# Four groups of GpSimd's element-wise work on VectorE, and an emission order that books the two engines as excluding each other

## The chip, the cores and the metric

The kernel runs on one core of one Trainium2 chip. TensorE (PE in the profile, its weight loads PEld), VectorE (DVE), ScalarE (ACT), GpSimd (POOL) and SyncE (SP) each work through a queue of their own in order, and semaphores make them wait for one another. DMA transfers are issued from the queues of SP, ACT and POOL. The metric is the device time of one execution in microseconds, as the median of several runs.

## The reference

One layer of a hybrid decoder over 1024 tokens of width 1024, all in float32, cut to what matters here:

```python
mod = silu(c) @ ada_w + ada_b
sh1, sc1, g1, sh2, sc2, g2 = split(mod, 6)
h = rms_norm(x, norm1_g) * (1 + sc1) + sh1
z = h @ w_in                                   # 1024 x 3896
y_fox = fox_mixer(z[:, :FOX_COLS])             # 8 heads of 64, attention with a forget gate
y_rwkv = rwkv7_mixer(z[:, FOX_COLS:])          # 8 heads of 64, a linear recurrence
x = x + g1 * (concat(y_fox, y_rwkv) @ w_out)
h = rms_norm(x, norm2_g) * (1 + sc2) + sh2
x = x + g2 * moe_ffn(h)                        # 64 experts of width 256, 6 per token, and a shared one
out = rms_norm(x, final_g)
# in fox_mixer, k and v are mixed with the token before:
k = a_k * shift_prev(k) + (1 - a_k) * k        # v the same with a_v; then rms_norm(k)
```

## The kernel before

Most float32 products are made as three matmuls of a high and a low part. For the weights of the input projection the function `halves` makes them: ScalarE copies the raw tile (`wraw`) into `whi` (L364), and L366 subtracts to get `wlo`, on VectorE for tile 1 and on GpSimd for the 30 others.

The projection (`proj`, L439) goes over 31 tiles of 128 columns: one of small columns, `wda`, `gd`, then r, k and v for each of four pairs of RWKV heads, four of the gate `fg`, and fk, fv and fq for each of four pairs of attention heads. Tile 0 is made at L428. Every other tile is 48 matmuls of 128x512 at L439, 1440 in all.

Around it run the other streams. For a pair of RWKV heads, in two halves each: `kappa` squares k (L630), sums the squares on TensorE (L602), takes inverse roots in a chain of tiny VectorE steps on the tile `hs` (`rstd_steps`, L152 to L164), spreads them (L610) and turns them back on TensorE (L617). `pre` makes two small products (L493). `main` scans (L671) and multiplies up to `fb` (L693), which the matmuls L698 read. `tok` transposes the results (L728). `inverse` inverts triangular blocks on VectorE (L773, L776), `merge` puts them together (L809, L820), and `chain` goes through 16 steps of the recurrence (L879 for its products, L910 to L943 for a step). For a pair of attention heads `fk` and `fv` mix with the token before (L1009 to L1013, L1037 to L1041); `fk` and `fq` normalise through the same chain (L602 to L617, on `sqk` and `sqq`). `rowmax` and `exps` are the attention (L1131 to L1177). `mods_gen` makes four rows of modulation from `ada_w`, partly on GpSimd (L1358, L1364). Then `project` (L1501 to L1505), `post` (L1523 to L1528, where h2 is made), `router`, `routes` (L1612, L1617), and the experts (L1853 to L1956), eight token blocks of the shared expert first.

The order in which all these are emitted, and so the order of each engine's queue, is made by `weave`. Each stream is a generator that emits some instructions and yields their estimated costs by engine; `weave` keeps for each engine the time at which it comes free, and always lets the stream go on whose time, less a lead of its own, is smallest. A cost that begins with `~` does not hold up its stream. The booking is

```python
t = free[e] = last = max(t, free.get(e, 0.0)) + c
```

Experts behind the eighth block yield nothing, so they are emitted in one piece, in an order of their own.

## Time and profile before

| | |
|---|---|
| median of 3 runs | 2192.78 us (2190.28 to 2195.71) |
| the profiled execution | 2183.48 us |
| its span | 2181.6 us |
| PE, DVE, ACT, POOL busy | 1906.9, 1477.0, 920.2, 974.0 us |
| granted TensorE clock, mean | 0.898 of full speed |

The page is one execution as the hardware profiler saw it. Busy is the time in which an engine has an instruction under way; waiting for a port inside an instruction counts as busy. The granted clock has two levels, 1.2 and 2.4 GHz, so 0.9 means a fifth of the time at the lower one.

### The profile page before, as it was taken

What the parts mean: (1) busy time and instruction counts of PE and PEld (TensorE: products, weight loads), DVE (VectorE), ACT (ScalarE), POOL (GpSimd) and SP (SyncE); (2) the same over time, 40 slices, a digit from 0 to 9 for tenths busy, and PEclk for the clock granted to TensorE, in tenths of its full rate; (3) what the DMA queues carried; (4) which work ended last, traced back from release to release, by engine and by line L of the source; (5) the groups of instructions that cost most, each with busy time, mean ns of one, the idle gap of its engine ahead of it and who ended that gap; (6) DMA issues with size and microseconds to landing.
All of it is one profiled execution on the core that took longest, in us unless ns stands there. A gap on an engine that the chain in (4) does not pass through costs nothing. (4 is left out here: it accounts for less than half of the span.)

```text
span 2181.6 us, 28292 instructions
## 1 busy us (share of the span) xinstructions
PE 1906.9 (87%) x9746; PEld 1427.8 (65%) x9746; DVE 1477.0 (68%) x2495; ACT 920.2 (42%) x1402; POOL 974.0 (45%) x702
## 2 busy tenths in 40 slices
PE   4898888888888788889988899999889899999993
PEld 3766666667676666555667678777667676666662
DVE  7736667773644656456576758777678788788884
ACT  5433433412222123244322335555456566556562
POOL 3322222212433324234366634664456656677762
PEclk7998786897978778799989999999999999999996
DMA  7124344555456266966464499999989999999975
GB/s 262 41 87 102 66 117 103 137 148 161 132 155 164 85 194 169 134 189 196 130 216 150 101 354 288 304 298 304 307 285 297 331 299 341 281 332 319 300 233 177
DMA packets 276770, 452.07 MB, mean 207 GB/s; under 512 B 132693, under 2 KB 202409, under 8 KB 250642
## 3 DMA queue, kind: packets, MB, share of 16 engines
q1 hardware_dynamic: 220578, 369.66, 52.4%
q0 software_dynamic: 24768, 66.75, 13.6%
q10 hardware_dynamic: 31280, 13.83, 2.4%
q8 instruction: 78, 1.28, 0.2%
q14 instruction: 66, 0.54, 0.1%
HBM read 355.27 MB, written 94.90 MB: 206 GB/s over the span
## 5 line engine op out<-in xcount | busy, mean ns | idle before, releaser
L1956 POOL DMA_INDIRECT d_acc<-ye,sl x84 | 198.0, 2357 | 288.1 <-DVE ye L1954 68.4
L366 POOL TENSOR_TENSOR wlo<-wraw,whi 128x1024 fp32r<-128x1024 f32 x30 | 79.7, 2656 | 356.4 <-ACT whi L364 356.4
L1888 POOL DMA_INDIRECT sl<-d_slot,d_sidx x84 | 190.9, 2273 | 27.6 <-issue 24.7
L1921 PE MATMUL gu<-guh,xh 128*128 128x512 f32 (+6 forms) x736 | 186.4, 396 | 1.6 <-ACT xh L1912 1.6
L1921 PE MATMUL gu<-guh,xl 128*128 128x512 f32 (+6 forms) x736 | 185.8, 394 | 0.1
L1921 PE MATMUL gu<-gul,xh 128*128 128x512 f32 (+6 forms) x736 | 185.4, 394 | 0.0
L1854 DVE TENSOR_TENSOR gul<-up,guh 128x1024 fp32r<-128x1024 f32 x128 | 155.8, 1217 | 10.6 <-ACT guh L1853 9.6
L1860 ACT ACTIVATE wdh<-down 128x1024 fp32r<-128x1024 f32 x128 | 128.6, 1052 | 72.2 <-PE yd L1921 72.2
L1921 PEld LDWEIGHTS gu<-guh,xh 128*128 128x128 f32 (+6 forms) x736 | 123.3, 168 | 50.0 <-ACT xh L1912 1.8
L1854 DVE TENSOR_TENSOR gul<-gate,guh 128x1024 fp32r<-128x1024 f32 x128 | 155.2, 1212 | 0.0
L1921 PEld LDWEIGHTS gu<-guh,xl 128*128 128x128 f32 (+6 forms) x736 | 121.8, 166 | 49.4 <-issue 1.2
L1921 PEld LDWEIGHTS gu<-gul,xh 128*128 128x128 f32 (+6 forms) x736 | 121.9, 166 | 47.6
L1861 DVE TENSOR_TENSOR wdl<-down,wdh 128x1024 fp32r<-128x1024 f32 x128 | 150.1, 1211 | 0.5
L439 PE MATMUL zp<-hTl,whi 128*128 128x512 f32 x480 | 148.5, 449 | 0.0
L1940 ACT ACTIVATE ah<-g 128x256 fp32r<-128x256 f32 (+5 forms) x92 | 31.3, 340 | 274.1 <-PE g L1938 274.1
L1896 POOL DMA_INDIRECT xg<-d_h,sl x84 | 135.3, 1611 | 25.6 <-issue 20.4
L439 PE MATMUL zp<-hTh,wlo 128*128 128x512 f32 x480 | 142.2, 434 | 0.0
L439 PE MATMUL zp<-hTh,whi 128*128 128x512 f32 x480 | 138.4, 429 | 0.0
L1853 ACT ACTIVATE guh<-gate 128x1024 fp32r<-128x1024 f32 x128 | 134.0, 1047 | 9.2 <-DMA gate<-in_exp_w_gate_dram 9.2
L1954 DVE SCALAR_TENSOR_TENSOR ye<-yd,sl,g 128x512 f32<-128x512 f32 (+12 forms) x168 | 119.9, 740 | 24.9 <-PE yd L1921 24.7
L1853 ACT ACTIVATE guh<-up 128x1024 fp32r<-128x1024 f32 x128 | 135.0, 1054 | 1.5 <-DMA up<-in_exp_w_up_dram 1.5
L1921 PE MATMUL yd<-wdh,ah 128*128 128x512 f32 (+6 forms) x368 | 128.2, 431 | 4.1 <-ACT ah L1940 2.3
(458 smaller groups left out, 4200.8 us busy)
## 6 DMA issues: line engine op xcount, KB each, us to landing
gate<-in_exp_w_gate_dram SPq DMA_DIRECT2D x64, 1024.0 KB
up<-in_exp_w_up_dram SPq DMA_DIRECT2D x64, 1024.0 KB
down<-in_exp_w_down_dram SPq DMA_DIRECT2D x64, 1024.0 KB
mw<-in_ada_w_dram SPq DMA_DIRECT2D x32, 512.0 KB
wraw<-in_w_in_dram SPq DMA_DIRECT2D x30, 512.0 KB
xw<-in_ada_w_dram SPq DMA_DIRECT2D x8, 1024.0 KB
xw<-in_x_dram SPq DMA_DIRECT2D x8, 512.0 KB
fb<-d_fb SPq DMA_DIRECT2D x16, 256.0 KB
```

The lines of the kernel that those rows point to most:

```text
L366: (nc.vector if j == 1 else nc.gpsimd).tensor_sub(lo, w, h.bitcast(F32))
L439: nc.tensor.matmul(z, a[:, d, :], b[:, d, hs], start=(n == 0 and d == 0), stop=(n == 2 and d == 7))
L1853: nc.scalar.activation(gh[:, qs, n, :], t[:, qs], AF.Copy)
L1854: nc.vector.tensor_sub(gl[:, qs, n, :], t[:, qs], gh[:, qs, n, :].bitcast(F32))
L1860: nc.scalar.activation(dh[:, j], raw[0][:, j], AF.Copy)
L1861: nc.vector.tensor_sub(dl[:, j], raw[0][:, j], dh[:, j].bitcast(F32))
L1888: nc.gpsimd.indirect_dma_start(out=sl[0:n], out_offset=None, in_=self.d_slot, in_offset=ind(idx[0:n]))
L1896: nc.gpsimd.indirect_dma_start(out=x[0:n], out_offset=None, in_=self.d_h2, in_offset=ind(ti))
L1921: nc.tensor.matmul(z, x[:, d, :], w[:, d, cs], start=(m == 0), stop=(m == 3 * n - 1))
L1940: nc.scalar.activation(ah[:, :, 0:n], tp[:, :, 0:n], AF.Copy)
L1954: nc.vector.scalar_tensor_tensor(y[0:n, hs], zs[h][0:n], wt, B["g2"][0:n, hs], op0=OP.mult, op1=OP.mult)
L1956: nc.gpsimd.indirect_dma_start(out=self.d_acc, out_offset=ind(ti), in_=y[0:n], in_offset=None, compute_op=OP.add)
```

## The change

Four groups of 128x1024 operations move from GpSimd to VectorE, 66 instructions in all: L366 for the 30 tiles that were left; L1358 and L1364 in `mods_gen` (12 and 4); L1009 in `fk` (4), L1037 and L1039 in `fv` (4 and 4); L1528 in `post` (8; the cost that `post` yields for it stays as it was, on POOL). In `weave` a cost may carry a star: then it is booked on its engine and also on one that is shared by all starred costs, so that starred VectorE and GpSimd work never overlaps in the plan. Nearly all element-wise costs of the two engines get a star (about 100 lines of the diff are nothing else); reductions, products that read PSUM and DMA work do not. Eleven of the leads are new. In the changed kernel, lines behind 1275 stand 9 further down.

```diff
-            (nc.vector if j == 1 else nc.gpsimd).tensor_sub(lo, w, h.bitcast(F32))
+            nc.vector.tensor_sub(lo, w, h.bitcast(F32))
...
-                    yield [("ACT", 1.0), ("POOL", 2.3)]
+                    yield [("ACT", 1.0), ("DVE*", 1.2)]
...
-                    yield [("DVE", .6), ("~POOL", 1.2)]
+                    yield [("DVE*", .6), ("~POOL*", 1.2)]
...
-                nc.gpsimd.tensor_sub(m, t[:, 0:T], t[:, 1:1 + T])
-                yield [("POOL", 2.3)]
-                nc.gpsimd.tensor_mul(m, m, ab)
-                yield [("POOL", 2.3)]
+                nc.vector.tensor_sub(m, t[:, 0:T], t[:, 1:1 + T])
+                yield [("DVE*", 1.15)]
+                nc.vector.tensor_mul(m, m, ab)
+                yield [("DVE*", 1.15)]
...
-                    (chain(), -1.2), (inverse(), 2), (merge(), 2), (zts(), -1.8), (prods(), 1.5), (feeds(), 4.8),
-                    (mixes(), 1.8), (kappa(), 1.2), (pre(), 1.2), (main(), 1),
+                    (chain(), -1.2), (inverse(), 2), (merge(), 2), (zts(), -1.8), (prods(), 1.5), (feeds(), 10.3),
+                    (mixes(), 12.6), (kappa(), 1.2), (pre(), 1), (main(), 1),
...
+        def book(e, t, c):
+
+            n, shared = e.rstrip("*"), e[-1] == "*"
+            t = max(t, free.get(n, 0.0), free.get("*", 0.0) if shared else 0.0) + c
+            free[n] = t
+            if shared:
+                free["*"] = t
+            return t
...
-                    last = free[e[1:]] = max(t, free.get(e[1:], 0.0)) + c
+                    last = book(e[1:], t, c)
...
-                    t = free[e] = last = max(t, free.get(e, 0.0)) + c
+                    t = last = book(e, t, c)
...
-                        nc.gpsimd.tensor_add(acc[1], acc[1], w)
-                        yield [("POOL", 2.3)]
+                        nc.vector.tensor_add(acc[1], acc[1], w)
+                        yield [("DVE*", 1.15)]
...
-            nc.gpsimd.tensor_add(acc[0], acc[0], acc[1])
-            yield [("POOL", 2.3)]
+            nc.vector.tensor_add(acc[0], acc[0], acc[1])
+            yield [("DVE*", 1.15)]
...
-                nc.gpsimd.tensor_add(h2, h2, mod[:, 0])
+                nc.vector.tensor_add(h2, h2, mod[:, 0])
```

What the new plan makes of the queues, at three places. First TensorE, the second pair of attention heads, from the sums of squares (L602 on `sqk`) to the turning back (L617). Before:

```order
L602 MATMUL g<-blk_123,sqk 128x2 x8
L439 MATMUL zp<-hTh,wlo 128x512 x4
L930 MATMUL pus<-xv,bk 64x64 x8
L439 MATMUL zp<-hTl,whi 128x512 x8
L439 MATMUL zp<-hTh,whi 128x512 x8
L937 MATMUL pm<-xv,gq 64x64 x8
L439 MATMUL zp<-hTh,wlo 128x512 x4
L617 MATMUL g<-idf,sqk 128x128 x4
```

In the changed kernel:

```order
L602 MATMUL g<-blk_123,sqk 128x2 x8
L439 MATMUL zp<-hTh,wlo 128x512 x4
L439 MATMUL zp<-hTl,whi 128x512 x8
L439 MATMUL zp<-hTh,whi 128x512 x8
L439 MATMUL zp<-hTh,wlo 128x512 x8
L439 MATMUL zp<-hTl,whi 128x512 x8
L439 MATMUL zp<-hTh,whi 128x512 x8
L439 MATMUL zp<-hTh,wlo 128x512 x8
L439 MATMUL zp<-hTl,whi 128x512 x4
L728 MATMUL g<-idf,mv 128x128 x4
L439 MATMUL zp<-hTl,whi 128x512 x4
L617 MATMUL g<-idf,sqk 128x128 x4
```

Between the two stood 24 projection matmuls and two groups of the recurrence; now there are 60 projection matmuls and a transpose of v. For the four pairs the counts of projection matmuls between are 12, 24, 24, 24 before and 24, 60, 52, 56 now in the order in which the pairs are numbered by the place of their L602; the row shown is the second.

Second TensorE, in the second pair of RWKV heads, from the L602 of the third pair's first half on. Before:

```order
L602 MATMUL g<-blk_123,sq 128x2 x4
L439 MATMUL zp<-hTl,whi 128x512 x4
L493 MATMUL ax<-wda,lora 128x512
L728 MATMUL g<-idf,b 128x128 x4
L439 MATMUL zp<-hTl,whi 128x512 x4
L809 MATMUL g<-z_1747,gx 32x32 x32
L728 MATMUL g<-idf,km 128x128 x4
L617 MATMUL g<-idf,sq 128x128 x4
L439 MATMUL zp<-hTh,whi 128x512 x4
L820 MATMUL g<-zt,z_1870 32x32 x32
L594 MATMUL g<-rk,blk 128x512
L493 MATMUL ax<-wda,lora 128x512
```

In the changed kernel, where the L617 of the second pair's second half stands two rows ahead of this piece:

```order
L602 MATMUL g<-blk_123,sq 128x2 x4
L493 MATMUL ax<-wda,lora 128x512
L617 MATMUL g<-idf,sq 128x128 x4
L493 MATMUL ax<-wda,lora 128x512
L602 MATMUL g<-blk_123,sq 128x2 x4
L809 MATMUL g<-z_1879,gx 32x32 x32
L493 MATMUL ax<-wda,lora 128x512
L698 MATMUL g<-fa,fb 64x64 x16
L820 MATMUL g<-zt,z_1970 32x32 x32
L728 MATMUL g<-idf,b 128x128 x4
L728 MATMUL g<-idf,km 128x128 x4
L617 MATMUL g<-idf,sq 128x128 x4
```

The projection matmuls that stood between these groups now stand in front of them. Counted in the same order, from the end of a pair's v projection to its first L698 there are 32, 100, 32 and 80 projection matmuls before and 44, 124, 40 and 164 now; from the end of its k projection to its first L602 12, 16, 16 and 16 before, 20, 16, 48 and 24 now. The first L910 stands behind 1016 of the 1440 before and 1224 now; the last L910 behind 32 and 51 of the attention's 96 products L1177; the first L1501 behind 78 and 96 of them. The gathers of the first two expert blocks on GpSimd stand one token block of the shared expert later.

Third VectorE, in the same chain of inverse roots as the first place (`hs` is its tile, 128x16). Before:

```order
L156 TENSOR_SCALAR hs_4174<-hs_4174 128x16
L157 TENSOR_SCALAR hs_4174<-hs_4174 128x16
L160 TENSOR_TENSOR hs_4174<-hs_4174 128x16
L162 TENSOR_TENSOR hs_4174<-hs_4174 128x16
L164 SCALAR_TENSOR_TENSOR hs_4174<-hs_4174 128x16
L160 TENSOR_TENSOR hs_4174<-hs_4174 128x16
L162 TENSOR_TENSOR hs_4174<-hs_4174 128x16
L164 SCALAR_TENSOR_TENSOR hs_4174<-hs_4174 128x16
L160 TENSOR_TENSOR hs_4174<-hs_4174 128x16
L162 TENSOR_TENSOR hs_4174<-hs_4174 128x16
L164 SCALAR_TENSOR_TENSOR hs_4174<-hs_4174 128x16
L610 COPY sqk<-hs_4174 128x1024
```

In the changed kernel:

```order
L162 TENSOR_TENSOR hs_3903<-hs_3903 128x16
L164 SCALAR_TENSOR_TENSOR hs_3776<-hs_3776 128x16
L773 TENSOR_TENSOR tmp<-z,xb 128x16x30
L366 TENSOR_TENSOR wlo<-wraw,whi 128x1024
L1037 TENSOR_TENSOR mv<-zs 128x1024
L164 SCALAR_TENSOR_TENSOR hs_3903<-hs_3903 128x16
L776 TENSOR_REDUCE z<-tmp 128x16
L160 TENSOR_TENSOR hs_3776<-hs_3776 128x16
L160 TENSOR_TENSOR hs_3903<-hs_3903 128x16
L773 TENSOR_TENSOR tmp<-z,xb 128x16x31
L162 TENSOR_TENSOR hs_3903<-hs_3903 128x16
L1039 TENSOR_TENSOR mv<-mv,abv 128x1024
```

A moved `wlo` and two moved operations of `fv` stand between the steps, and so do steps of the last inverse, which were done by then before.

## Rows read from the trace of the kernel before

**Rows 1.** The page's part on busy time: each engine's busy us, its share of the span, its instructions.

```profile
PE 1906.9 (87%) x9746; PEld 1427.8 (65%) x9746; DVE 1477.0 (68%) x2495; ACT 920.2 (42%) x1402; POOL 974.0 (45%) x702
```

**Rows 2.** The table of stages, us from the span's start: length, then busy us of PE, PEld, DVE, ACT and POOL with the number of instructions, PE's granted clock, the DMA engines' share, GB/s.

```profile
67.00:500.00 433.00, 363.39 (x1940) 279.16 (x1939) 278.20 (x511) 158.12 (x231) 94.45 (x85) 0.86 0.41 103
500.00:790.00 290.00, 248.45 (x1524) 197.42 (x1523) 154.51 (x235) 69.22 (x106) 107.41 (x83) 0.82 0.51 141
790.00:1065.00 275.00, 246.36 (x1350) 163.19 (x1350) 144.64 (x334) 100.31 (x196) 92.77 (x97) 0.85 0.66 167
1065.00:1260.00 195.00, 167.38 (x836) 135.79 (x835) 139.68 (x397) 53.25 (x84) 121.82 (x152) 0.93 0.56 171
1260.00:2150.00 890.00, 846.24 (x3957) 623.38 (x3955) 696.80 (x901) 499.32 (x725) 527.12 (x252) 0.98 0.92 297
```

**Rows 3.** The waits of PE from 67 to 500 us: instruction, what it waited for, us in total, times, the longest.

```profile
PE g L698 <- DVE fb L693: 21.2, 5, 9.2
PE g L602 <- ACT sq L630: 14.4, 3, 8.4
PE g L602 <- ACT sqk L1017: 7.3, 1, 7.3
PE g L617 <- DVE sq L610: 6.9, 6, 2.7
PE g L698 <- DVE hs L162: 5.6, 1, 5.6
PE ax L585 <- DVE b L575: 5.5, 1, 5.5
```

**Rows 4.** The same from 500 to 790 us.

```profile
PE g L617 <- DVE sqk L610: 23.3, 4, 8.2
PE g L617 <- DVE sqq L610: 8.9, 2, 4.5
```

**Rows 5.** The same from 1065 to 1260 us.

```profile
PE g L1617 <- DVE Mb L1612: 9.1, 5, 3.2
PE g L1544 <- POOL h L1528: 6.5, 3, 3.9
```

**Rows 6.** The timeline from 567 to 579 us: start, length, engine, line, operation, names, shapes; in brackets the idle time before and what ended it.

```profile
567.37 0.17 DVE L162 TENSOR_TENSOR hs<-hs 128x16 f32<-128x16 f32 x1
567.74 2.00 PE L439 MATMUL zp<-hTh,whi 128*128 128x512 f32 x8
...
567.96 2.38 POOL L1358 TENSOR_TENSOR macc<-macc,mw 128x1024 f32<-128x1024 f32 x1 [11.21 <-PE zp L439]
567.99 2.39 DVE L162 TENSOR_TENSOR hs<-hs 128x16 f32<-128x16 f32 x1
570.31 2.37 POOL L366 TENSOR_TENSOR wlo<-wraw,whi 128x1024 fp32r<-128x1024 f32 x1
570.42 2.29 DVE L164 SCALAR_TENSOR_TENSOR hs<-hs 128x16 f32<-128x16 f32 x1
...
572.63 1.89 POOL L1037 TENSOR_TENSOR mv<-zs 128x1024 f32<-128x1024 f32 x1
572.74 1.82 DVE L160 TENSOR_TENSOR hs<-hs 128x16 f32<-128x16 f32 x1
574.49 2.34 POOL L1364 TENSOR_TENSOR macc<-macc,macc 128x1024 f32<-128x1024 f32 x1
574.59 2.26 DVE L162 TENSOR_TENSOR hs<-hs 128x16 f32<-128x16 f32 x1
...
577.94 1.09 PE L617 MATMUL g<-idf,sqk 128*128 128x128 f32 x4 [6.18 <-DVE sqk L610]
```

**Rows 7.** Four of the seven moved lines, each line's own view: number, shortest, median and longest duration in ns, first and last start, shapes.

```profile
L366 POOL TENSOR_TENSOR wlo<-wraw,whi x30: 2339/2386/6884, 36.7 to 719.3; 128x1024 fp32r<-128x1024 f32 x30
L1358 POOL TENSOR_TENSOR macc<-macc,mw x12: 2335/2372/3800, 541.7 to 839.7; 128x1024 f32<-128x1024 f32 x12
L1528 POOL TENSOR_TENSOR h<-h,mod x8: 2382/2405/3374, 1062.6 to 1191.5; 128x1024 f32<-128x1024 f32 x8
L1037 POOL TENSOR_TENSOR mv<-zs x4: 1893/1900/1915, 499.9 to 750.6; 128x1024 f32<-128x1024 f32 x4
```

**Rows 8.** An operation of that shape on VectorE, L1011, in the same view.

```profile
L1011 DVE TENSOR_TENSOR mk<-mk,abk x4: 1208/1218/1564, 490.9 to 729.5; 128x1024 f32<-128x1024 f32 x4
```

**Rows 9.** The timeline at the first and the last of the 43 VectorE instructions that are held beside one of the 66.

```profile
95.70 2.68 POOL L366 TENSOR_TENSOR wlo<-wraw,whi 128x1024 fp32r<-128x1024 f32 x1 [8.33 <-ACT whi L364]
96.15 2.54 DVE L567 CAST km<-mv 32x512 fp32r<-32x512 f32 x1
...
1191.46 2.40 POOL L1528 TENSOR_TENSOR h<-h,mod 128x1024 f32<-128x1024 f32 x1
1193.37 1.58 DVE L1905 TENSOR_TENSOR xl<-xg,xh 128x1024 fp32r<-128x1024 f32 x1 [1.67 <-ACT xh L1904]
```

**Rows 10.** The timeline of the front, 34 to 48 us.

```profile
39.48 6.99 PE L294 MATMUL mp<-ones,acc 128*128 128x1 f32 x32 [14.10 <-DVE acc L284]
```

**Rows 11.** The timeline from 126 to 134 us, PE alone.

```profile
127.69 0.97 PE L602 MATMUL g<-blk,sq 128*128 128x2 f32 x8
132.17 0.66 PE L617 MATMUL g<-idf,sq 128*128 128x128 f32 x4 [0.65 <-DVE sq L610]
```

**Rows 12.** The table of stages for a stretch behind two waits, columns as in rows 2.

```profile
505.80:522.80 17.00, 16.06 (x155) 13.61 (x156) 4.55 (x5) 4.61 (x7) 0.00 (x0) 0.50 0.31 94
```

More of the change, by code (lines that the diff above doesn't have):

```diff
@@ L146, in rstd_pow @@
         nc.gpsimd.tensor_tensor(r, x, self.mhalf.to_broadcast(list(r.shape)), op=OP.pow)
-        yield [("POOL", .4 + .165 * r.shape[-1])]
+        yield [("POOL*", .4 + .165 * r.shape[-1])]
     def rstd_steps(self, r, x, tmp, n, eps):
@@ L300, in cols @@
                                                op0=OP.add, op1=OP.mult)
-                yield [("DVE", .07)]
+                yield [("DVE*", .07)]
                 yield [("set", ("md", h))]
@@ L310, in split @@
                 self.columns(pp)
-                yield [("PE", .1), ("DVE", .5)]
+                yield [("PE", .1), ("DVE*", .5)]
                 for d in range(8):
@@ L487, in setup @@
             nc.vector.tensor_scalar(zi, zj, 0.0, None, op0=OP.is_equal)
-            yield [("DVE", .5)]
+            yield [("DVE*", .5)]
         def mm(lhsT, rhs, hs):
@@ L506, in mixes @@
                 mix(j)
-                yield [("DVE", 1.2)]
+                yield [("DVE*", 1.2)]
                 kind, p = tiles[j]
@@ L557, in gates @@
             nc.vector.tensor_copy(w3[32:64], w)
-            yield [("DVE", 1.0)]
+            yield [("DVE*", 1.0)]
             nc.vector.tensor_sub(w.bitcast(F32R), w, w3[32:64].bitcast(F32))
@@ L561, in gates @@
             nc.vector.tensor_copy(w3[64:96], w.bitcast(F32R))
-            yield [("DVE", 1.5)]
+            yield [("DVE*", 1.5)]
             sg = M["small", 0][32:64]
@@ L713, in main @@
                     F[p, h, "o"] = b, km, rk
-                    yield [("POOL", 2.5)]
+                    yield [("POOL*", 2.5)]
                     yield [("set", ("half", 2 * p + h))]
@@ L960, in ynorm @@
                 nc.vector.tensor_scalar(s[:, 0], s[:, 0], -1.0 / 64, None, op0=OP.mult)
-                yield [("DVE", .1)]
+                yield [("DVE*", .1)]
                 nc.gpsimd.tensor_add(y, y, b8(s[:, 0]))
-                yield [("POOL", 1.3)]
+                yield [("POOL*", 1.3)]
                 sq = rp.tile([128, 8, 64], F32, name="sq", bufs=1)
@@ L989, in parts @@
             put(x, lo)
-            yield [("DVE", 1.15)]
+            yield [("DVE*", 1.15)]
         def fgate():
@@ L1363, in mods_gen @@
             nc.sync.dma_start(row, A["ada_b"][0:1, c0:c0 + D])
-            nc.gpsimd.tensor_add(acc[0], acc[0], acc[1])
-            yield [("POOL", 2.3)]
+            nc.vector.tensor_add(acc[0], acc[0], acc[1])
+            yield [("DVE*", 1.15)]
             for h in range(2):
@@ L1410, in weights @@
                 nc.gpsimd.tensor_mul(raw, raw, g1)
-                yield [("POOL", 2.3)]
+                yield [("POOL*", 2.3)]
                 nc.scalar.activation(hi, raw, AF.Copy)
@@ L1414, in weights @@
                 nc.vector.tensor_sub(lo, raw, hi.bitcast(F32))
-                yield [("DVE", 1.1)]
+                yield [("DVE*", 1.1)]
                 wo.append((hi, lo))
@@ L1569, in route @@
             nc.vector.tensor_add(sel, sc, rb)
-            yield [("DVE", .14)]
+            yield [("DVE*", .14)]
             m8 = t("m8", [128, 8, 8])
@@ L1576, in route @@
             nc.vector.tensor_add(gs, m8[:, :, 0], m8[:, :, 1])
-            yield [("DVE", .08)]
+            yield [("DVE*", .08)]
             v8 = t("v8", [128, 8])
@@ L1585, in route @@
             nc.vector.tensor_copy(xf, x8)
-            yield [("DVE", .07)]
+            yield [("DVE*", .07)]
             e4 = t("e4", [128, 8, 4])
@@ L1589, in route @@
                                     xf[:, None, 0:4].to_broadcast([128, 8, 4]), op=OP.is_equal)
-            yield [("DVE", .1)]
+            yield [("DVE*", .1)]
             gm = t("gm", [128, 8])
@@ L1603, in route @@
             nc.vector.tensor_copy(xf, x8)
-            yield [("DVE", .07)]
+            yield [("DVE*", .07)]
             oh = t("oh", [128, K_SEL, NE])
@@ L1612, in route @@
                 nc.vector.tensor_reduce(Mb[:, i, :], oh.rearrange("q k e -> q e k"), op=OP.add, axis=AX.X)
-            yield [("~POOL", 1.0), ("DVE", .47)]
+            yield [("~POOL*", 1.0), ("DVE", .47)]
             pos = pg.tile([128, 512], F32, name="g")[:, 0:NE]
@@ L1661, in route_consts @@
             nc.vector.tensor_copy(self.tok, self.toki)
-            yield [("POOL", 1.0), ("DVE", .5)]
+            yield [("POOL", 1.0), ("DVE*", .5)]
             z = tp.tile([128, D], F32, name="z0")
@@ L1719, in ranks @@
         nc.vector.scalar_tensor_tensor(a, crow[0:NE], pk[:, 1:2], a, op0=OP.is_gt, op1=OP.add)
-        yield [("DVE", .45)]
+        yield [("DVE*", .45)]
         rank = t("rank", [NE, 1])
@@ L1727, in ranks @@
         nc.vector.tensor_copy(eb, pk[:, 0:1].to_broadcast([NE, 128]))
-        yield [("DVE", .4)]
+        yield [("DVE*", .4)]
         po = ps()
@@ L1756, in leftover @@
         nc.vector.tensor_scalar(j8, i64[0:NE, 0:8], 128.0, rem, op0=OP.mult, op1=OP.is_lt)
-        yield [("DVE", .15)]
+        yield [("DVE*", .15)]
         nov = t("nov", [NE, 1])
@@ L1761, in leftover @@
         nc.vector.tensor_scalar(lt2, i64[0:NE], self.tok[0:NE, 0:1], None, op0=OP.is_gt)
-        yield [("DVE", .2)]
+        yield [("DVE*", .2)]
         pc = ps()
@@ L1772, in leftover @@
         nc.vector.tensor_scalar(dd, dd, cs, None, op0=OP.subtract)
-        yield [("POOL", .3), ("DVE", .3)]
+        yield [("POOL", .3), ("DVE*", .3)]
         va = t("va", [NE, 128])
@@ L1783, in leftover @@
         nc.vector.tensor_copy(rb_, rk[:, 0:1].to_broadcast([NE, 128]))
-        yield [("DVE", .3)]
+        yield [("DVE*", .3)]
         pe = ps()
@@ L1882, in shared @@
                             nc.vector.tensor_sub(l, raw[:, qs], h.bitcast(F32))
-                        yield [("~POOL", 2.3) if q else ("~DVE", 1.15)]
+                        yield [("~POOL*", 2.3) if q else ("~DVE*", 1.15)]
             yield [("set", ("shared w", 0))]
@@ L2065, in experts @@
                     if b < 8:
-                        yield [("~ACT", 1.0), ("~DVE", 1.2)]
+                        yield [("~ACT", 1.0), ("~DVE*", 1.2)]
                 if act is not None:
```

113 lines of the change are left out of this document (57 added, 56 removed).

## The prediction

> **What bounds the kernel now.** I read the page's busy table first: PE 1906.9 of 2181.6 us, DVE 1477.0, POOL 974.0 [rows 1]. A share over stages with different limits decides nothing, so the table of stages comes next [rows 2]. From 1260 us on, PE works 846 of 890 us at a granted clock of 0.98 of full speed. Those are the experts; their code is emitted in one piece and the change leaves its order alone, so I count nothing there. From 67 to 1260 us PE is idle for 69.6 + 41.5 + 28.6 + 27.6 = 167 us, and its clock is 0.86, 0.82, 0.85 and 0.93. PE runs one queue in order and holds all the stages' matmuls, so this part of the program lasts as long as PE's work, plus its waits, plus what half speed costs. At 0.86 of full speed 28% of a stage is spent at half speed; over the four stages that makes 121 + 104 + 83 + 27 = 335 us, and half of it, 167 us, is lost wherever PE has work throughout.
>
> Third, what ends PE's waits. From 67 to 500 us it is VectorE's product fb (L693), the squares that ScalarE takes (L630, L1017), the spread inverse roots (L610) and the gates' copies [rows 3]. From 500 to 790 us it is nearly the normalisation alone: sqk 23.3 and sqq 8.9 us [rows 4]. In the routing stage it is the one-hot counts and GpSimd's sum h2 [rows 5]. So PE waits mostly for VectorE, while VectorE is only 64%, 53% and 53% busy [rows 2]: it is not full, it is late at certain places.
>
> Fourth, why it is late there. At 567 us VectorE runs a chain of tiny operations on hs at 0.17 us each. Then GpSimd starts four 128x1024 operations in a row, L1358, L366, L1037 and L1364, and four of VectorE's tiny ones last 2.39, 2.29, 1.82 and 2.26 us: 8.8 us in place of 0.7. PE's transpose behind the chain has waited 6.18 us when it starts [rows 6]. All four are instructions that the change takes from GpSimd.
>
> **The change, part by part.** *The 66 moved instructions.* On GpSimd they are 30 of L366 at a median 2.39 us, 12 of L1358 at 2.37, 8 of L1528 at 2.41, 4 of L1037 at 1.90 [rows 7]; the 4 of L1009 are like L1037 and the 4 each of L1039 and L1364 like L1358, an estimate. That is 72 + 28 + 19 + 8 + 8 + 19 = 154 us less on GpSimd, which no wait of PE needs except in routing: worth nothing by itself. On VectorE one such operation takes 1.22 us [rows 8], so 66 add 80 us. Against that stands what they hold up today. Beside 43 of VectorE's instructions that last longer than others of their shape stands one of the 66, and the surplus adds up to 77 us; the first is a cast at 96.15 us, the last a subtraction at 1193.37 us that takes 1.58 us for 1.22 [rows 9]. VectorE's total so comes out even (+3 us). The gain is in where the time lies: a held instruction is late at a place that the order did not foresee, a moved one stands in a place of its own.
>
> Here a rule of the Trainium skill bears on the sum. The row shows a VectorE instruction of 0.17 us lasting as long as GpSimd's beside it [rows 6]. "SBUF — State Buffer", section "Who interferes with whom", says that the two engines share a pair of ports that is locked for a whole instruction, so the later one waits to its end. By that rule alone each of the 66 could hold VectorE, 66 x 2.3 = 152 us, and the move would free 72 us net, an estimate from that page; the trace shows about half of that held, and the sum goes by the 77 us. The rule that speaks against the change is a rival below.
>
> *Normalisation, 500 to 790 us:* waits of 32.2 us [rows 4]. Two things act. The held chains get shorter: 8.8 us held at the place shown, for a wait of 6.18. And PE has more to do meanwhile: between L602 and L617 of the four sqk stand 24, 60, 52 and 56 projection matmuls instead of 12, 24, 24 and 24. Eight take 1.98 to 2.00 us at full speed [rows 6], so the 12 to 36 more are worth 3 to 9 us each, against waits of 3.5 to 8.2 us. Bounds 0 to -32; I take **-27**, since the moved instructions also stand within these chains now (one wlo and two of fv in the second, some 3.6 us, among steps of the last inverse).
>
> *fb before L698:* 21.2 + 5.6 us [rows 3]. From the end of a pair's v projection to its L698 there are 44, 124, 40 and 164 projection matmuls for 32, 100, 32 and 80 before, so 2 to 21 us more cover for waits of up to 9.2 us. Bounds +5 to -27; I take **-15**. *The squares before L602:* 14.4 + 7.3 us [rows 3]; 20, 16, 48 and 24 matmuls for 12, 16, 16 and 16, and the subtraction L1009 in front of sqk takes 1.22 us on VectorE. Bounds 0 to -22; **-8**. *The gates' copies and sq:* 5.5 + 6.9 us [rows 3]; three more wlo (3.7 us) stand in front of the gates on VectorE, where held instructions such as the cast of 2.54 us go. Bounds +4 to -12; **-5**. *Routing:* 9.1 + 6.5 us [rows 5]; h2's sum goes from 2.4 to 1.2 us and no longer holds VectorE in the stage. Bounds 0 to -15; **-8**. *The front:* wlo of the first tile stands on VectorE ahead of the last eight accumulations, for which PE waits 14.10 us [rows 10]; nothing hides its 1.2 us: **+1**.
>
> *What the new order lays bare.* In the second pair (the second order excerpt), L617, L602, L698 and the four transposes stand on PE with no projection matmul between, because the projections of that pair are done by then. A normalisation with nothing in its way takes 3.5 us from the end of L602 to L617 [rows 11]; one of these pairs of groups has a single L493 between, the other six small groups. L698 has only small groups since the L617 that feeds it, and the longest wait for it today is 9.2 us [rows 3]. Queued behind are tok and the third pair's projections. Bounds 4 to 20 us; **+12**. The chain's first L910 stands behind 1224 of 1440 projection matmuls instead of 1016, and the gathers of the first experts later by about one token block of the shared expert: bounds 0 to 20, **+5**.
>
> The waits so change by -27 - 15 - 8 - 5 - 8 + 1 + 12 + 5 = **-45 us**.
>
> *Half speed.* From 505.8 to 522.8 us, behind two waits, the clock is at 0.50 throughout [rows 12]. Today 167 us of waits go with 167 us lost that way, one for one. Bounds 0 to -45 for the 45 us. *Given back.* A PE that comes sooner and runs faster meets its next results less ready: chains on VectorE, ScalarE and the queues do not shorten with it. Bounds 0 to all of the 90. I take half, since VectorE is little over half busy and the covers grew at most places: -90 + 45 = **-45 us**.
>
> The profiled execution took 2183.5 us (span 2181.6 plus 1.9 outside it), so 2138.5; it lies 9.3 us under the median of the runs, 2192.8. The prediction in terms of that median is **2148 us**.
>
> **The rivals.** *Nothing changes, 2193 us.* For it: VectorE's total is even by the sum above, and GpSimd was not the bound. The Trainium skill says so of such moves: "Perfetto Trace Analysis", section "Optimizing Scalar/DVE Operations", warns that operations offloaded between GpSimd and VectorE might not help because they share a read port. By that rule the sum is 0. Against: PE's waits name single late results, and the rows show what makes them late.
>
> *Slower, 2213 us.* The place is the second and third pair and the chain. VectorE's queue is in order: a wlo there waits for whi on ScalarE, which waits for the weights and for the projection two tiles back, and scan, fb and the inverse's steps queue behind it. If the inverses end later, the chain of 16 steps does. Its last step stands behind 51 of the attention's 96 L1177 products instead of 32, and the output projection, behind 78 of them before and all 96 now, must wait for it. Price: 20 us, the upper bound of the bare place, with the rest of the gain given back. It decides from the point where PE's waits between 67 and 1260 us come to more than today's 167 us. Against: VectorE is 53% busy from 500 to 790 us.
>
> *Much faster, 2103 us.* Little is given back: all 90 us. For it: the covers grew at nearly every place counted. Against: no plan of this sort is met to the microsecond.
>
> **How the numbers follow.** A difference of 0.3% (6.6 us) is about what this kernel's runs can tell from none. Chances: the forecast (2120 to 2175) 0.55, much faster 0.20, nothing 0.11, slower 0.14. Faster by over 0.3% is 0.55 + 0.20 + 0.02 = 0.77, the same 0.08, slower 0.14 + 0.01 = 0.15. The range reaches to the other cases and leaves out a tenth on each side: 2092 to 2203 us.
>
> **What would show it.** Right: PE's waits for sqk and sqq from 32 to under 8 us; no tiny hs instruction of over 2 us beside a 128x1024 GpSimd one; GpSimd busy about 150 us less; VectorE's busy time within 15 us of 1477; the clock from 500 to 790 us above 0.86; a bare stretch of some 12 us in the second pair. Wrong: PE's idle time ahead of the routed experts is not 20 us lower; or VectorE idles in front of L366 for ScalarE by more than 30 us in all, which would make the second rival the cause.

## The result, and the profile after

| | before | changed |
|---|---|---|
| median | 2191.53 us (2181.34 to 2195.71, 4 runs) | 2117.97 us (2111.28 to 2122.39, 4 runs) |
| the profiled execution | 2183.48 us | 2122.39 us |

The changed kernel takes 0.9668 of the time before, with a 95% interval of 0.9623 to 0.9714: 73.6 us less by the medians, where the prediction said 45. The profiled executions lie 61.1 us apart, since that of before was one of the faster and that of the changed kernel the slowest of the four; what follows accounts for the 61.

Busy time of the changed kernel, as in [rows 1]:

```profile
PE 1857.9 (88%) x9746; PEld 1395.1 (66%) x9746; DVE 1468.6 (69%) x2561; ACT 919.9 (43%) x1400; POOL 844.7 (40%) x636
```

Its stages, columns as in [rows 2]; below them two stretches that follow the work and not the clock on the wall, from the first projection matmul to the first transpose of a routed expert's tokens, and from there to the last expert product:

```profile
67.00:500.00 433.00, 388.70 (x2098) 299.72 (x2098) 282.99 (x546) 164.77 (x240) 38.98 (x61) 0.87 0.44 111
500.00:790.00 290.00, 249.49 (x1674) 194.05 (x1672) 172.84 (x333) 84.04 (x143) 55.80 (x72) 0.86 0.58 159
790.00:1065.00 275.00, 232.70 (x1309) 162.38 (x1310) 162.89 (x359) 98.09 (x180) 102.22 (x105) 0.90 0.72 189
1065.00:1260.00 195.00, 171.46 (x858) 140.35 (x858) 125.89 (x354) 55.82 (x88) 98.88 (x131) 0.95 0.62 193
68.50:1214.80 1146.30, 995.66 (x5712) 757.96 (x5710) 716.52 (x1550) 385.24 (x621) 279.42 (x355) 0.88 0.56 149
1214.80:2086.80 872.00, 827.76 (x3892) 608.94 (x3890) 687.50 (x890) 494.90 (x719) 540.89 (x245) 0.97 0.92 296
```

The same two stretches of the kernel before:

```profile
66.70:1277.50 1210.80, 1042.51 (x5712) 789.13 (x5710) 725.92 (x1485) 386.14 (x624) 424.60 (x421) 0.86 0.52 141
1277.50:2148.00 870.50, 829.57 (x3890) 610.06 (x3890) 687.47 (x890) 494.38 (x718) 518.07 (x245) 0.98 0.92 296
```

The experts take 872.0 us for 870.5: nothing happened there, as foreseen. The stretch before them is 64.5 us shorter (1146.3 for 1210.8). Of these, PE's idle time is 17.7 us (150.6 for 168.3, length less PE's busy time), and 46.8 us is PE's busy time, for the same 5712 instructions: they ran faster, at a granted clock of 0.88 for 0.86. Counted between the instants at which the trace's granted clock changes, PE is busy for 292.4 us at the lower level before and for 198.4 us in the changed kernel. Work lasts twice as long there (eight projection matmuls 3.78 us at 282.3 us of the changed kernel, 1.98 us at 218.3), so half of the difference of 94.0 us, 47.0, is what the clock gave back: the whole fall. The fixed stages show how far the work has moved ahead: the last projection matmul starts at 663 us in place of 784, the first attention product at 673 in place of 790, so the stage from 790 to 1065 us holds other work than in [rows 2].

PE's waits in the first of the two stretches, to be read beside [rows 3 to 5]:

```profile
PE g L602 <- ACT sqk L1017: 17.8, 4, 14.4
PE pm L910 <- ACT yt L943: 12.8, 2, 11.9
PE s L1186 <- ACT os L1182: 12.1, 9, 4.0
PE s L1143 <- DVE mm L1139: 11.6, 6, 7.1
PE g L617 <- DVE sq L610: 8.8, 3, 4.8
PE s L1164 <- ACT qk L1144: 8.7, 7, 3.9
PE s L1164 <- ACT pT L1169: 6.2, 2, 5.9
PE g L1553 <- ACT r_sc L1563: 5.0, 3, 2.3
PE g L602 <- ACT sqq L1056: 4.6, 2, 4.3
PE g L602 <- ACT sq L630: 3.0, 3, 2.4
PE g L1626 <- DVE Mb L1621: 2.9, 2, 1.5
PE zp L439 <- ACT whi L364: 2.3, 1, 2.3
```

Two lines of the same view of the kernel before, for waits that [rows 3 to 5] do not show:

```profile
PE s L1143 <- DVE mm L1139: 2.3, 1, 2.3
PE s L1164 <- ACT pT L1169: 2.1, 4, 1.5
```

What the prediction aimed at is gone. L617 waited 32.2 us for sqk and sqq [rows 4]; 1.1 us for sqk is left of it. L698 waited 26.8 us [rows 3] and waits no more. L602's wait for the squares of the RWKV pairs went from 14.4 to 3.0 us, L1617 (L1626 now) for the one-hot counts from 9.1 to 2.9. Against that stand new or longer waits: L602's for sqk 17.8 us for 7.3, of which the first is 14.4 us in one piece, yt 12.8, mm 11.6 for 2.3, os 12.1, qk and pT 14.9, of which pT was 2.1 (os and qk were 1.6 together, yt nothing). Added up by line and cause over the whole view, 113 us of waits went and 95 came, which leaves 17.5 of the 17.7.

### The profile page after: what moved, and what is told of

Same layout as the page of the kernel before. It is cut to its first block, busy times and chain, and to the rows that moved or that the text cites. A ratio compares the mean times of both kernels' runs of the same rounds, so it can differ in the third digit from the quotient of the medians.

```text
span 2120.5 us, 28237 instructions
## 1 busy us (share of the span) xinstructions
PE 1857.9 (88%) x9746; PEld 1395.1 (66%) x9746; DVE 1468.6 (69%) x2561; ACT 919.9 (43%) x1400; POOL 844.7 (40%) x636
## 5 line engine op out<-in xcount | busy, mean ns | idle before, releaser
L1897 POOL DMA_INDIRECT sl<-d_slot,d_sidx x84 | 221.8, 2640 | 27.5 <-issue 25.0
L1862 ACT ACTIVATE guh<-gate 128x1024 fp32r<-128x1024 f32 x128 | 134.0, 1047 | 17.5 <-DMA gate<-in_exp_w_gate_dram 17.5
L1905 POOL DMA_INDIRECT xg<-d_h,sl x84 | 125.5, 1494 | 25.8 <-issue 19.8
L439 PE MATMUL zp<-hTl,whi 128*128 128x512 f32 x480 | 131.4, 410 | 0.0
L1919 PE MATMUL tp<-idf,xg 128*128 128x128 f32 (+11 forms) x672 | 94.6, 286 | 40.0 <-DMA xg<-d_h,sl 40.0
L439 PE MATMUL zp<-hTh,wlo 128*128 128x512 f32 x480 | 129.3, 407 | 0.0
```

What stands on the lines that cost most here:

```text
L439: nc.tensor.matmul(z, a[:, d, :], b[:, d, hs], start=(n == 0 and d == 0), stop=(n == 2 and d == 7))
L1862: nc.scalar.activation(gh[:, qs, n, :], t[:, qs], AF.Copy)
L1897: nc.gpsimd.indirect_dma_start(out=sl[0:n], out_offset=None, in_=self.d_slot, in_offset=ind(idx[0:n]))
L1905: nc.gpsimd.indirect_dma_start(out=x[0:n], out_offset=None, in_=self.d_h2, in_offset=ind(ti))
L1919: nc.tensor.transpose(tp[:, j, 0:n], x[0:n, 4 * q + j:D:8], self.idf[0:n, 0:n])
```

## The experiments

All ratios are to runs of the kernel before on the same chip (median 2179 to 2184 us there for the experiments), with the 95% interval; one per cent is 22 us. The experiments ran on two chips, so they are compared by their ratios. Where the intervals of two rows overlap, the difference between the two is not settled by them. "Old order" is that of the kernel before, "new plan" means that the moved operations are booked at VectorE's cost.

| | operations on | booking | leads | median us | ratio |
|---|---|---|---|---|---|
| e1 | VectorE | old order | old | 2162.9 | 0.991 (0.9875 to 0.9945) |
| e2 | GpSimd | new plan, shared | new | 2116.8 | 0.968 (0.965 to 0.972) |
| changed | VectorE | new plan, shared | new | 2118.0 | 0.967 (0.962 to 0.971) |
| e3 | VectorE | new plan, shared | old | 2154.8 | 0.987 (0.983 to 0.991) |
| e8 | GpSimd | new plan, shared | old | 2168.9 | 0.992 (0.989 to 0.996) |
| e4 | VectorE | new plan, apart | new | 2161.5 | 0.991 (0.987 to 0.995) |
| e5 | VectorE | new plan, apart | old | 2135.3 | 0.977 (0.971 to 0.983) |
| e12 | GpSimd | new plan, apart | old | 2163.8 | 0.990 (0.987 to 0.994) |
| e6 | VectorE | new plan, shared | front ones old | 2184.1 | 1.002 (0.998 to 1.006) |
| e7 | VectorE | new plan, shared | tail ones old | 2140.5 | 0.979 (0.971 to 0.987) |

**Is it the engine or the order?** The prediction's theory was that a held VectorE instruction is late at a place that counts, and that more matmuls stand in PE's queue meanwhile; it never separated the two. The first run moves the operations and leaves the order as it was; the second leaves them on GpSimd and takes the new order.

```diff
-            (nc.vector if j == 1 else nc.gpsimd).tensor_sub(lo, w, h.bitcast(F32))
+            nc.vector.tensor_sub(lo, w, h.bitcast(F32))
...
-                nc.gpsimd.tensor_add(h2, h2, mod[:, 0])
+                nc.vector.tensor_add(h2, h2, mod[:, 0])
```

(and so the other lines moved, in the kernel before, with no cost that is yielded touched; the second run is the reverse edit in the changed kernel.)

> The kernel before with one edit: the 66 operations are issued on VectorE, all yielded costs, the planner and the leads as before, so the order in which the program emits its instructions is that of before, to the instruction. Engine theory (the gain is that GpSimd no longer holds VectorE up): the surplus of 77.6 us beside the 66 goes to under 10, PE's waits for sqk and sqq from 32 to about 15 us, and the time to 2150 to 2170 us. Order theory (the gain is in the new order, the engine matters little): 2185 to 2200 us, waits for sqk and sqq still over 25 us. Third theory (moved operations in places that were chosen for GpSimd get in the way of VectorE's chains; the change needs both): slower than before, 2200 us or more.

> The changed kernel with one edit: the 66 operations are issued on GpSimd again, all yielded costs, the planner and the leads as in the changed kernel, so the order is that of the changed kernel. Engine theory: VectorE's instructions beside the 66 are held again by some 70 us, and of the 74 us gained at least 40 are lost: 2155 to 2185 us. Order theory: at most 20 us are lost: 2118 to 2138 us. Third theory (needs both): nearly all is lost, 2180 us or more.

Measured: 2162.9 us for the first, 0.9% faster than before, and 2116.8 for the second, which cannot be told from the changed kernel. The first, PE's waits and the stretch up to the routed experts:

```profile
PE g L698 <- DVE fb L693: 19.9, 4, 9.1
PE g L602 <- ACT sq L630: 17.0, 4, 7.3
PE g L617 <- DVE sqk L610: 10.9, 4, 4.5
PE g L617 <- DVE sqq L610: 6.7, 3, 2.4
...
68.00:1245.00 1177.00, 1013.07 (x5713) 765.79 (x5711) 719.07 (x1551) 386.35 (x624) 276.37 (x355) 0.89 0.54 146
```

The surplus beside the 66 is gone, and L617's waits for sqk and sqq fell from 32.2 to 17.6 us, as the engine theory asked; L698 and the squares, whose cover (the projection matmuls queued ahead) is the old one, wait as before. PE's idle time as a whole fell by only 4.4 us (163.9 for 168.3): other waits grew, L617's for sq from 6.9 to 13.5. So the engine is worth 0.9% in the old order, some 20 us by the ratio (16 by the medians) and less than a third of the gain. Now the second, GpSimd and VectorE from 594 to 603 us and PE at 615, with its busy times ahead:

```profile
PE 1861.1 (88%) x9746; PEld 1397.9 (66%) x9746; DVE 1467.1 (69%) x2495; ACT 919.5 (43%) x1400; POOL 991.9 (47%) x702
...
594.46 2.41 POOL L366 TENSOR_TENSOR wlo<-wraw,whi 128x1024 fp32r<-128x1024 f32 x1 [13.30 <-ACT whi L364]
595.60 1.30 DVE L164 SCALAR_TENSOR_TENSOR hs<-hs 128x16 f32<-128x16 f32 x1
596.86 3.41 POOL L1367 TENSOR_TENSOR macc<-macc,mw 128x1024 f32<-128x1024 f32 x1
597.96 2.34 DVE L160 TENSOR_TENSOR hs<-hs 128x16 f32<-128x16 f32 x1
600.33 0.17 DVE L162 TENSOR_TENSOR hs<-hs 128x16 f32<-128x16 f32 x1
600.35 2.43 POOL L1373 TENSOR_TENSOR macc<-macc,macc 128x1024 f32<-128x1024 f32 x1
600.54 2.27 DVE L164 SCALAR_TENSOR_TENSOR hs<-hs 128x16 f32<-128x16 f32 x1
...
615.57 0.66 PE L617 MATMUL g<-idf,sqq 128*128 128x128 f32 x4
```

Beside L366, L1367 and L1373 on GpSimd three of VectorE's hs steps last 1.30, 2.34 and 2.27 us where others take 0.17, just as in [rows 6]. In all, 43 of its instructions are held beside the 66 for 75.6 us (over 0.3 us more than the median of their shape); the same count gives 43 for 77.0 us before. But the L617 behind this chain stands at 615.57 with no wait: 104 projection matmuls are queued between its L602 and it. Before, the same L617 had 52 and waited 4.5 us, the longest for sqq in [rows 4]; in the first run it had the same 52 and waited 2.1. So in the changed order the held instructions cost nothing that the time shows: the two ratios differ by 0.15%, 3 us, which their intervals make 3 give or take 13. The order theory stands for the changed order. That the cover is what makes the difference fits this chain; it is not shown by it, and the last run on the engine below speaks against it.

**Which part of the order?** Four runs take back the leads, the booking, or both. In the run without booking the star is ignored; the one with both is the changed kernel with these two edits.

```diff
-            n, shared = e.rstrip("*"), e[-1] == "*"
+            n, shared = e.rstrip("*"), False
```
```diff
-                    (chain(), -1.2), (inverse(), 2), (merge(), 2), (zts(), -1.8), (prods(), 1.5), (feeds(), 10.3),
-                    (mixes(), 12.6), (kappa(), 1.2), (pre(), 1), (main(), 1),
+                    (chain(), -1.2), (inverse(), 2), (merge(), 2), (zts(), -1.8), (prods(), 1.5), (feeds(), 4.8),
+                    (mixes(), 1.8), (kappa(), 1.2), (pre(), 1.2), (main(), 1),
...
```

> The changed kernel with the eleven leads of before; the operations on VectorE, the booking with the shared engine kept. If moving and booking carry the gain, 2118 to 2145 us. If the new leads carry it, 2165 us or more. My forecast is 2140 us: the leads decide where projection matmuls stand between L602 and L617, which is worth some 3 to 9 us for each pair.

> The changed kernel with one edit: the star is ignored, so that VectorE and GpSimd are booked apart; operations on VectorE and new leads kept. If the booking matters by itself, GpSimd's operations are planned to overlap VectorE's chains again and the time is 2135 us or more. If what is left on GpSimd is too little to hold up VectorE at a place that counts, 2110 to 2130 us, no clear difference. My forecast is 2125 us.

> The changed kernel with the eleven leads of before and with the star ignored: what is left of the change is that the 66 operations are on VectorE and are booked there at 1.15 to 1.2 us in place of 2.3 on GpSimd. Its order puts 44, 12, 44 and 32 projection matmuls between L602 and L617 of the four sqk. If the booking or the leads each bring a part by themselves, this one is the slowest of the family, 2165 to 2185 us, near the kernel with the old order and the operations on VectorE (2163). If booking and leads count only together, it is like the one without booking and the one with the old leads, 2150 to 2165 us. My forecast is 2165 us.

The first two lose 2.0 and 2.4% against the changed kernel, more than forecast for either; the first falls between its two cases, the second into the one in which the booking matters. The third was a surprise: with neither booking nor new leads it is 1.0 and 1.4% faster than with one of them alone, where it was expected to be the slowest (its four runs took 2129.6 to 2137.4 us, the least of either of the others on the same chip 2152.6). Booking alone costs, the leads alone cost, both together gain 1.0% (these two intervals just touch): these leads fit the plan with booking and hurt in the other. Some two thirds of the whole gain (2.3 of 3.3%) are there with the operations and their booked costs alone, with the old leads.

> The changed kernel with six of the eleven leads as before, those of streams that run beside the projection (feeds, mixes, pre, loader, fgate, fv). The kernel with all eleven old lost 38 us against the changed one; its trace has 14 us more of L1626 in the routing stage, 9 us of L698 that the changed one has not, and 8 us more for the first sqk. If the front leads carry the loss, 2140 us or more; if the tail leads do, 2115 to 2130 us. My forecast is 2135 us: the waits for L698 and the first sqk belong to the front.

> The changed kernel with the other five leads as before, those of the stage swaps, of ynorm and of the router. If they carry the loss of 38 us, 2140 us or more, with some 14 us of waits at L1626 as in the kernel with all leads old; if the front leads do, 2115 to 2125 us. My forecast is 2132 us.

```diff
-                    (tok(), 2), (setup(), 0), (gates(), -0.5), (loader(), 0), (weights(), 3.3),
-                    (fgate(), 1.8), (fk(), 1.8), (fv(), 0.8), (fq(), -0.5), (proj(), 0.6),
+                    (tok(), 2), (setup(), 0), (gates(), -0.5), (loader(), 0.8), (weights(), 3.3),
+                    (fgate(), 1.6), (fk(), 1.8), (fv(), -0.2), (fq(), -0.5), (proj(), 0.6),
...
```

The diff is the second half of the first run's edit; feeds, mixes and pre change with it, and the other run has the remaining five (ynorm, swap_ff, router, swap_fox_out, swap_project). Both runs pass the 2140 us that was named for them, the second narrowly and with 15.8 us of waits at L1626 where some 14 were foretold. So neither set carries the loss alone, and the forecasts (2135 and 2132) were low. Without the six leads beside the projection 3.5% are lost and the kernel is no faster than before; without the other five 1.2%, with intervals that just overlap. Six old leads are worse than all eleven (1.002 for 0.987), so a lead has no worth of its own either. Which single lead does it, and by which wait, stays open.

**Where the engine still counts.** Two runs put the operations back on GpSimd under the two other plans.

```diff
-            nc.vector.tensor_sub(lo, w, h.bitcast(F32))
+            (nc.vector if j == 1 else nc.gpsimd).tensor_sub(lo, w, h.bitcast(F32))
...
```

(and so the other lines moved.)

> The kernel with the old leads and the booking (2155 us), with the 66 operations issued on GpSimd. In the old order the engine is worth some 18 us, in the changed order nothing. If it is the cover by projection matmuls that makes the held instructions harmless, and that cover comes with the new costs and the booking (52, 60, 16 and 16 matmuls between L602 and L617 of the four sqk, two of them short), the engine counts here in part: 2158 to 2168 us. If the new leads make them harmless, it counts in full: 2170 us or more. If the operations' engine never mattered under a new plan: 2150 to 2158 us. My forecast is 2160 us.

> The kernel with old leads and no booking (2135 us, its operations on VectorE) with the 66 operations issued on GpSimd, in the same order. So far the engine was worth 18 us in the old order, 14 us with booking and old leads, and nothing in the changed order. If a held instruction costs by how far its consumer is covered, this order with 12 to 44 projection matmuls between L602 and L617 stands between: 2140 to 2155 us. If moving the operations is what replanning alone needs, 2160 us or more. If the engine does not matter once the plan is new, 2130 to 2140 us. My forecast is 2145 us.

They lose 0.5 and 1.3%. So the engine is worth some 20 us in the old order, 11 with booking and old leads, 29 with the costs alone, and nothing that can be measured in the changed one. The 20 and the 29 are clear of their intervals; the 11 is not (the two intervals overlap between 0.989 and 0.991), and it cannot be told from the changed order's 3. The first of the two runs, forecast at 2160, came out at 2169, at the edge of the case in which the engine counts in full; the second, forecast at 2145, is in the case in which replanning needs the operations moved. The counts between L602 and L617 do not foretell this: the run with 12 to 44 matmuls there was forecast to lose 10 us, and it lost 29; and in its trace the L617 with 12 ahead of it waits for nothing, the one with 32 for 4.4 us. Its stretch up to the routed experts, first with the operations on VectorE (e5), then on GpSimd (e12):

```profile
69.00:1235.10 1166.10, 1015.06 (x5711) 771.99 (x5710) 711.35 (x1549) 385.92 (x623) 269.45 (x355) 0.87 0.55 146
```

```profile
67.00:1266.80 1199.80, 1032.66 (x5710) 782.74 (x5709) 700.39 (x1484) 386.04 (x623) 425.35 (x421) 0.86 0.53 142
```

PE's idle time is 16 us more (167.1 for 151.0), its busy time 17.6 more; the execution profiled with GpSimd was the slowest of its six, so the two together are somewhat more than the 29 us. Which held instruction does it the runs do not show: no line's wait for one thing grew by more than 4.9 us.

**What waits now.** Two of the new waits of the changed kernel stand behind a load. At 440 us, lines of SyncE, VectorE, ScalarE and PE:

```profile
431.31 0.53 SPq L853 DMA_DIRECT2D fb<-d_fb  x1
443.58 1.18 SPq L978 DMA_DIRECT2D abk<-d_ak  x2
448.33 1.23 DVE L1011 TENSOR_TENSOR mk<-mk,abk 128x1024 f32<-128x1024 f32 x1 [10.90 <-DMA abk<-d_ak]
453.06 1.06 ACT L1017 ACTIVATE sqk<-mk 128x1024 f32<-128x1024 f32 x1 [15.72 <-DVE mk L1013]
454.17 2.08 PE L602 MATMUL g<-blk,sqk 128*128 128x2 f32 x9 [14.42 <-ACT sqk L1017]
```

VectorE needs abk for L1011; its load is issued on SyncE's queue at 443.58, behind eighteen loads of the chain since 431 us. The first edit issues this pair's four loads from ScalarE's queue, the second does the same with the rows mw of the modulation, the third has both.

```diff
-                nc.sync.dma_start(t[R[a]], self.d_ak[r0 + a:r0 + a + 1, :].to_broadcast([64, T]))
+                q = nc.scalar if r0 in (0, 8) else nc.sync
+                q.dma_start(t[R[a]], self.d_ak[r0 + a:r0 + a + 1, :].to_broadcast([64, T]))
```
```diff
-                nc.sync.dma_start(w, A["ada_w"][0, k * 128:(k + 1) * 128, c0:c0 + D])
+                nc.scalar.dma_start(w, A["ada_w"][0, k * 128:(k + 1) * 128, c0:c0 + D])
```

> The changed kernel with the first pair's four loads of the mixing rows (abk, abv) issued from ScalarE's queue in place of SyncE's, where they stand behind the chain's loads. In the changed kernel PE waits 14.4 us in one piece at 440 us for the first sqk, VectorE's L1011 ahead of it 10.9 us for abk. If the late load makes the wait, it falls to under 5 us, and the time by 10 to 20 us (half speed included): 2098 to 2110 us. If the next result is as late, the wait moves on and the time stays within 6 us of 2118.

> The changed kernel with the loads of mw (32, of 512 KB each) issued from ScalarE's queue in place of SyncE's. In the changed kernel ScalarE and VectorE stand idle for 9.6 and 8.2 us at 786 and 804 us behind a product with mw that has not landed; PE waits 11.95 us there for yt, which ScalarE copies behind it, and 7.1 us for mm; the clock is at half speed from 789 to 820 us. If the late load on a full queue makes these waits, both fall by half or more and the time by 10 to 25 us: 2093 to 2108 us. If ScalarE now waits for a free buffer at its own DMA issues instead, no gain, or up to 10 us slower.

> Both edits of the loads in one kernel. If each removes a wait of its own, at 440 us and at 786 us, the gains add up: 2080 to 2100 us. If what is gained early is given back later, the time is that of the better of the two.

The first gives what its first case said, 2102.5 us, a ratio of 0.9625 (0.9588 to 0.9662), the best of all here; the interval overlaps with that of the changed kernel (0.9623 to 0.9714), so that it is better is likely and not settled. The same place in it (its lines behind 978 stand one further down):

```profile
426.67 1.70 ACTq L979 DMA_DIRECT2D abk<-d_ak  x2
436.29 1.22 DVE L1012 TENSOR_TENSOR mk<-mk,abk 128x1024 f32<-128x1024 f32 x1
442.42 1.06 ACT L1018 ACTIVATE sqk<-mk 128x1024 f32<-128x1024 f32 x1 [4.82 <-DVE mk L1014]
443.53 2.72 PE L602 MATMUL g<-blk,sqk 128*128 128x2 f32 x12 [4.57 <-ACT sqk L1018]
```

The loads go out at 426.67 and the wait is 4.57 us for 14.42; L602 waits for sqk 9.2 us in all, for 17.8. The second edit gives 2119.2 us, 0.9695 (0.9667 to 0.9723): no gain. In the changed kernel, then with the edit (L1351, L1358 and L1364 are lines of these kernels, the load and two products with mw, none of them among the 66; the moved lines L1358 and L1364 of before are L1367 and L1373 here):

```profile
790.25 1.62 SPq L1351 DMA_DIRECT2D mw<-in_ada_w_dram  x2
795.85 1.15 ACT L1364 ACTIVATE mw<-mw,sc 128x1024 f32<-128x1024 f32 x1 [9.59 <-issue]
797.02 0.77 ACT L943 ACTIVATE yt<-pm 64x256 f32<-64x256 f32 x2
797.84 3.68 PE L910 MATMUL pm<-xv,st 128*128 128x64 f32 x16 [11.95 <-ACT yt L943]
```

```profile
794.62 0.74 DVE L1358 TENSOR_SCALAR macc<-mw,sc 128x1024 f32<-128x1024 f32 x1
795.39 0.91 ACTq L1351 DMA_DIRECT2D mw<-in_ada_w_dram  x2
802.21 1.15 ACT L1364 ACTIVATE mw<-mw,sc 128x1024 f32<-128x1024 f32 x1 [6.27 <-DMA mw<-in_ada_w_dram]
803.38 0.77 ACT L943 ACTIVATE yt<-pm 64x256 f32<-64x256 f32 x2
```

ScalarE stands 9.59 us in front of L1364 and copies yt (L943) only behind it; PE's L910 waits 11.95 us. The profile names no releaser there ("issue"); that it is the load issued at 790.25 is inferred from the order of the loads. With the edit the load goes out at 795.39, as soon as L1358 is through with its buffer; its product starts 6.8 us later, and ScalarE still waits 6.27 us for it. So a free buffer and the load's own time are what is left, more than the queue. PE's waits for yt and mm fell from 24.4 to 16.5 us in all, those for os rose from 12.1 to 18.1, and the kernel's time shows neither. Both together give 2108.7 us, 0.9654 (0.9627 to 0.968), between the two and told from neither by the intervals.

## Why the prediction was right, and where it was not

The direction held; of the two reasons, more matmuls queued ahead of a late result and no held VectorE instructions, only the new order as a whole was needed in the changed kernel, which the prediction did not separate. The size was short by 29 us, and the measured 2118 lies just under the forecast's own band (2120 to 2175), nearer to the case "much faster" (2103). Step by step:

- *What bounds the kernel.* Right: the gain is all ahead of the routed experts, in waits of PE and in its clock.
- *The 66 instructions.* VectorE's busy time is 1468.6 us, even as worked out (1477.0); GpSimd's fell by 129 us and not 154, for its indirect gathers of slots took 221.8 us (L1897, 84 of them) where they took 190.9 before. "The gain is in where the time lies" is half right: it describes the old order, where the move alone brings 20 us. In the changed order the move brings nothing that can be measured, as the second run shows. The rule of the Trainium skill that stood against the change, "Perfetto Trace Analysis", section "Optimizing Scalar/DVE Operations" (an offload between the two engines may not help), agrees with that run, and does not hold for the 20 and the 29 us in two other orders.
- *Normalisation, -27.* The covered waits went from 32.2 to 1.1 us. But L602's own waits for sqk and sqq rose from 8.2 to 22.4 us (17.8 + 4.6); the sum had sqk's in the squares, as a gain, and sqq's in no term. Ahead of the first sqk it was a load on SyncE's queue that VectorE waited for. *fb, -15:* it was -26.8, all of it. *The squares, -8:* -0.9, for sq fell by 11.4 and sqk rose by 10.5. *Gates and sq, -5:* 12.4 to 10.0 (1.2 + 8.8). *Routing, -8:* 15.6 to 7.9 (2.9, and 5.0 at L1553 for r_sc where it was h). *The later chain, +5:* 12.8 us for yt alone, most of it behind the product with mw and not because the chain stands later. *The front, +1:* PE's gap there grew by 1.7 us.
- *Bare place, +12.* Too large as a wait. From 239.9 to 287.7 us the changed kernel goes through the bare groups, in its longest stretch at the lower clock; below it, the same time of the kernel before, which holds other work:

```profile
239.90:287.70 47.80, 41.68 (x233) 26.11 (x232) 26.06 (x62) 22.70 (x33) 5.14 (x8) 0.50 0.55 124
```

```profile
239.90:287.70 47.80, 44.02 (x299) 30.41 (x299) 23.12 (x52) 22.46 (x33) 10.83 (x11) 0.72 0.49 110
```

PE's idle time there is 6.1 us, so no wait of 12 us. What the bare place costs besides is speed, which the term did not have; how much, two rows of different work do not tell.
- *Half speed and given back: the step that failed.* I let the speed follow the waits one for one and then took half of both away, which makes 22.5 us of waits and 22.5 us of speed. The waits came out near that, by 17.7 us, though not by way of the terms: 95 of 113 us came back, chiefly in the attention and at the first sqk. The speed was mis-sized: PE's busy time fell by 46.8 us, twice the term. The rate of one for one came from two totals that happened to be equal, and no row showed it. The 167 us of lost speed was itself too high: of 341 us at the lower clock PE worked in 292, so 146 us were lost. The traces show where the two part: up to the routed experts the lower clock came in 37 stretches before and in 19 now, and 67.9 us of PE's idle time lie within them, for 49.0 before. So more of the waiting that is left falls where the clock is low already. Why the number of stretches halved while the idle time fell by a tenth is not shown. So the direction was no luck; that the forecast came as near as it did is in part luck, for single waits came out far from their terms and the errors cancelled.
- *The rivals.* "Nothing changes" is out. "Slower" is out, and yet its sign was there. VectorE's idle time in front of L366:

```profile
DVE wlo L366 <- ACT whi L364: 53.1, 19, 13.3
```

53 us of idleness, well over the 30 I had set, and PE's matmuls behind it waited for nothing but a whi, for 2.3 us. Idle time of an engine that nobody waits for was a bad sign to choose. So was the other: PE's idle time fell by 17.7 us, under the 20 that I had asked for, and the kernel was faster all the same. Of the signs for "right", the clock from 500 to 790 us only reached 0.86, and GpSimd's busy time fell by 129 us for the 150.

## What to carry to other kernels

When a change moves instructions and the plan at once, run the move in the old order and the new order without the move; here that showed within two runs that the new order made the gain with the operations on either engine. What the move is worth depends on the order (3 to 29 us in four of them), and counting the matmuls ahead of one consumer did not foretell it. Leads fitted to one plan cost 1.4% under another here: after a change to the costs they have to be fitted again, and the losses from taking back two sets of them did not add up, so none can be judged alone. And when the waits named by a profile are covered, look at what a late load stands behind on a shared DMA queue next; the best run here came from moving four small loads, though its lead over the changed kernel is not settled.

## What the runs showed of the hardware

**Length is work, waits and clock.** Over the stretch up to the routed experts, take from its length PE's idle time (length less busy time) and what half speed cost, (1 - clock) of the length: the rest is nearly the same in kernels whose length differs by 80 us: before 1210.8 - 168.3 - 0.14 x 1210.8 = 873 us, changed 858, e1 884, e2 873, e5 863, e12 865, e6 852, e9 870. So the two columns account for a kernel's length to about 2%. Cut at the instants where the trace's granted clock changes, it is closer: PE's busy time, less half of what falls at the lower level, is 893 to 901 us in the traces of before, changed, e1 to e9 and e12 (before 896.3, changed 896.5). But idle time and clock don't go together one for one: e1 has 4 us less idle time than before and a clock of 0.89 for 0.86.

**One program, two clocks.** The kernel before ran 19 times beside the first four experiments: 2168.9 to 2199.6 us, at mean clocks of 0.897 to 0.907, the longer runs at the lower clock as a rule (a fall of some 17 us for each 0.01). The profiled execution of e1 was the one at the highest clock of its ten (0.914; median 0.907). A single profile therefore says of the clock's share only to within some 15 us what a change did; the ratios above are from medians.
